# A hybrid decoder block with a PEER feed-forward on one core: six row buffers from the start, half-size weight loads, a first query projection in two pieces, and gate constants on early-free memory

## The chip, the cores and the metric

The kernel runs on one core of a Trainium2 chip. The metric is the device time in microseconds (us) of one launch. One launch was also profiled; its rows are quoted below. PE is the matmul engine (TensorE), DVE is VectorE, ACT is ScalarE, POOL is GpSimd and SP is SyncE, which here only issues transfers.

## The reference

One decoder block over 1024 tokens of width 1024: two token mixers (a stick-breaking attention and a gated delta net, 8 heads each) run on the normed input, are merged through sigmoid gates and go through an output projection into the residual stream. Then comes a PEER feed-forward: 16,384 single-neuron experts, addressed by two keys of 128 (e1 and e2).

```
h = rms_norm(x);  proj = h @ w_in
x = x + (sigmoid(gate_sb) * (o_sb @ w_branch_sb) + sigmoid(gate_gdn) * (o_gdn @ w_branch_gdn)) @ w_out
h2 = rms_norm(x)
q = h2 @ peer_w_q                                # 8 heads x 2 halves x 128
s1, s2 = q_half1 @ keys1.T, q_half2 @ keys2.T    # 128 scores each, top 16 of each
vals, c = top_k(s1 + s2, 16);  expert = e1 * 128 + e2;  gate = softmax(vals)
act = gelu(h2 . peer_u[expert]);  x = x + sum(gate * act * peer_v[expert])
```

Each token uses 8 x 16 = 128 experts. All of it is float32.

## The kernel before

**Tiling.** Tokens go in blocks of 128 and in two halves of four blocks (512 tokens). Float32 operands are split into a high and a low part (`split`: ACT makes the high part, DVE the low one), and each product is three matmuls (`mm3`, L72 to L74: high*high, high*low, low*high).

**Order.** Half 0, then half 1: `mixers` (attention heads, L295 to L317, then the delta net), gate logits, `merge`, `out_proj`, `ffn_norm` with `norm_T` (L678 to L686: norm a token block into `n_h`, transpose it on PE into `hf`), and `route` (per head: query projection `mm<-w,hf`, scores `pz<-keysT,r_q`, and on DVE a top 16 by `r_v`, `r_ix`). `route_block` turns the tops of a block into expert numbers and gates.

**Two ways for the experts.** Four of the eight token blocks go the dense way, the other four the gathered way.

- The *dense pass* handles four blocks (2, 3, 6, 7) against all experts: for each e1, `scores` (L885, L887: 128 experts' dot products on PE, then gelu), `weigh` (times the gate, into `d_a`), and on PE the products with the value rows `d_v` (`pz<-d_v,d_a`); after each four e1 and each half of the width DVE adds the sums to `d_acc` (L974). Its gates come from a *gate table* (`gate_table`): 64 steps of 8 tokens build a 128 x 128 gate matrix per token from one-hot tiles `gt_o`, and write it to memory as `g_d`. `gate_consts` makes a constant `gt_R` (4096 wide) and two small ones, `gt_L0` and `gt_L1`; the tile `gt_er` goes by DMA into `gt_L`, and PE multiplies `gt_R` by `gt_L` (L835).
- The *gathered* blocks (0, 1, 4, 5) fetch per token one row of 1024 floats for each of their 128 experts: POOL issues an indirect DMA (L1016, 128 tokens x 4 KB = 512 KB) into a row buffer `gb_row`, and DVE does one instruction of 1024 elements on it: a dot product for a `peer_u` row (L1019), a multiply-add into `gb_h` for a `peer_v` row (L1021). A block is 128 u rows and then 128 v rows; there are 1024 in all.

**What places the rows.** Rows of the first half's blocks can be gathered from half 1 on. `gather(phase)` is called at fixed places of each stage; it adds `PACE[phase]` to a count and creates as many row instructions as the count allows, at low priority: a scheduler puts every engine's instructions in order ahead of time, so a row may land later in DVE's order than its call. A row buffer is used in turn: four tiles, `gb_row0` to `gb_row3`; only in the dense pass two more are added (pool `gp2`). A row's DMA can start when DVE has finished the row that had the same buffer.

**Weights.** `load_w` brings 256 columns of a weight matrix as two DMAs of 512 KB (four blocks of 128 rows each) into `w_raw`, which has two buffers, and splits each in two steps (w_hi on ACT, w_lo on DVE). SP issues these loads in order, each when its buffer is free.

```
PACE = dict(sb=2.2, gdn=1.5, logits=2.5, merge=2.5, out=0.5, route=0, table=0.1, dense=5.25)
        self.due += PACE[phase]
        self.anchor = self.last_dve()
        with self.later(1000000):
            while self.due >= 1:
                self.due -= 1
                next(self.rows, None)
```

Of the kernel before, what the change touches and what calls it, by code (L numbers as in the profile page):

```python
# [30 lines left out]
PACE = dict(sb=2.2, gdn=1.5, logits=2.5, merge=2.5, out=0.5, route=0, table=0.1, dense=5.25)  # L31
# [7 lines left out]
class Block:  # L39
# [60 lines left out]
    def load_ba(self):  # L100

        hi, lo = [self.wp.tile([P, KD, CB], F32R, name=f"w_{a}")[:, :, 0:16] for a in ("hi", "lo")]
        raw = self.wraw.tile([P, 4, CB], F32, name="w_raw").rearrange("p a b -> p (a b)")[:, 0:16 * KD]
# [237 lines left out]
    def sb_pair(self, half, pair, kqv):  # L341
        nc = self.nc
        k, q, v = kqv
        for h in range(2):
            kts = [k[:, h, j * P:(j + 1) * P] for j in range(NTB)]
            vs = [v[:, j, h * P:(h + 1) * P] for j in range(NTB)]
            if half:
                ko = self.ch.tile([P, TH], F32, name="ko", bufs=2)
                nc.sync.dma_start(ko, self.k_old[pair][:, h])
                vo = self.ch.tile([P, NTB, P], F32, name="vo", bufs=2)  # L350
# [100 lines left out]
    def gdn_head(self, half, head, G, r):  # L451
# [247 lines left out]
    def route(self, half, hx, pool):  # L699
# [4 lines left out]
        for h in range(H):  # L704
            w = self.load_w(self.i["peer_w_q"], h * CB)
            q = []
            for t in range(2):
                ps = self.pmm.tile([P, TH], F32, name="mm")
                self.proj_T(ps, w, hx, t)
# [95 lines left out]
    def gate_table(self, n, blk, pool):  # L805
# [7 lines left out]
        tr = pool.tile([P, 3, P], F32, name="gt_tr", bufs=2)  # L813
        nc.scalar.copy(tr[:, 0:2], ps)
        nc.vector.tensor_scalar(tr[:, 2], tr[:, 1], -1.0, None, op0=OP.mult)
        er = pool.tile([P, 2, P], F32R, name="gt_er", bufs=2)
        nc.vector.tensor_scalar(er[:, 0], self.ef[blk][1], -64.0, None, op0=OP.add)
        nc.vector.tensor_tensor(er[:, 1], er[:, 0].bitcast(F32), er[:, 0].bitcast(F32), op=OP.mult)
# [360 lines left out]
```

## Time and profile before

| | |
|---|---|
| median of 3 runs | 3883.02 us (3879.04 to 3883.69) |
| the profiled execution | 3877.26 us, its span 3875.4 us |
| PE busy | 3596.4 us, 93% of the span |
| DVE busy | 3077.5 us, 79% |
| ACT busy | 1740.7 us, 45% |
| POOL busy | 1356.6 us, 35% |
| mean granted PE clock | 0.971 of full speed |
| data moved | 937.49 MB, 242 GB/s over the span; 536.94 MB of it by the gathered rows' queue |

Shares are of the whole span; the stages differ, and a table by stage stands first among the rows below; a window's row gives its start and end, its length, and the busy time of PE, PEld (PE's weight loads), DVE, ACT and POOL, each with its count of instructions. From 1010 us on the row gathering runs beside everything else. The stages, by the instructions that begin them: half 0 to 850 us, its norm and route to 1010, attention of half 1 to 1400, delta net to 1770, gate logits and merge to 1905, output projection and norm to 2010, route to 2127, gate table to 2400, dense pass to 3853, and a tail of last rows.

### The profile page before, as it was taken

To read this page: it belongs to the slowest core of one execution; us is meant where nothing else is said; L and a number is where in the kernel's file an instruction comes from. 1 tells how busy PE (TensorE), PEld (TensorE's weight loads), DVE (VectorE), ACT (ScalarE), POOL (GpSimd) and SP (SyncE) were. 2 spreads that over 40 slices of the span, in tenths; PEclk is the share of its full clock that TensorE was granted. 3 is DMA by queue.
4 is the path that set the end of the run, shared out by engine and by line. 5 is a ranking of instruction groups with operands and counts; after the bars stand their busy time and mean duration, and the time that the engine had idled before them with its cause. 6 is when DMAs were issued, how large, how long until landed. Compare 5 with 4: busy or idle time off the path is not lost.

```text
span 3875.4 us, 53560 instructions
## 1 busy us (share of the span) xinstructions
PE 3596.4 (93%) x18936; PEld 2983.8 (77%) x18936; DVE 3077.5 (79%) x6196; ACT 1740.7 (45%) x3846; POOL 1356.6 (35%) x1034
## 2 busy tenths in 40 slices
PE   8999999999999999998878877999999999999996
PEld 7878888788777688886667666787778787788785
DVE  5345554349988878888879998899898899899898
ACT  6755554333777655553322786222222322222221
POOL 0000000000044332223442003666666665676665
PEclk9999999999999999999989999999999999999998
DMA  4221113553377756558985568999999999999998
GB/s 121 88 82 50 55 50 115 174 186 93 96 256 265 246 191 192 191 182 290 325 307 170 158 185 289 353 361 358 334 365 358 345 371 365 348 364 374 353 359 312
DMA packets 344205, 937.49 MB, mean 242 GB/s; under 512 B 41984, under 2 KB 121088, under 8 KB 339712
## 3 DMA queue, kind: packets, MB, share of 16 engines
q0 software_dynamic: 147456, 536.94, 38.8%
q1 hardware_dynamic: 196480, 397.13, 30.1%
q8 instruction: 149, 2.44, 0.3%
q14 instruction: 120, 0.98, 0.1%
HBM read 864.22 MB, written 69.21 MB: 241 GB/s over the span
## 4 chain that ended last, share of the span: by engine, by line
PE 42%; issue 20%; POOL 12%; DVE 11%; DMA 10%; ACT 4%; SPq 0%; POOLq 0%; DVEq 0%; ACTq 0%
POOL gb_row L1016 12%; PE mm L72 6%; PE mm L74 6%; PE mm L73 6%; DMA gb_row<-peer_v,expert 5%; PE pc L848 3%; DMA gb_row<-peer_u,expert 3%; PE mm L885 2%; PE pz L532 2%; PE pz L526 2%; DVE gb_row L1019 2%; DVE w_lo L64 2%; PE mm L887 1%; PE pc L317 1%; PE pz L295 1%
## 5 line engine op out<-in xcount | busy, mean ns | idle before, releaser
L1016 POOL DMA_INDIRECT gb_row<-peer_u,expert x512 | 693.6, 1355 | 1848.2 <-DVE expert L793 1012.8
L1016 POOL DMA_INDIRECT gb_row<-peer_v,expert x512 | 661.9, 1293 | 656.4 <-DVE gb_h L1021 408.8
L1019 DVE SCALAR_TENSOR_TENSOR gb_row<-gb_row,gb_h 128x1024 f32<-128x1024 f32 x512 | 614.0, 1219 | 133.2 <-DMA gb_row<-peer_u,expert 109.7
L1021 DVE SCALAR_TENSOR_TENSOR gb_h<-gb_row,gb_act,gb_h 128x1024 f32<-128x1024 f32 x512 | 657.7, 1285 | 73.7 <-DMA gb_row<-peer_v,expert 50.4
L885 PE MATMUL mm<-hf,ut 128*128 128x512 f32 x2048 | 491.2, 391 | 6.9 <-DMA hf<-hd 6.9
L919 ACT CAST d_a<-u_act 128x512 fp32r<-128x512 f32 x128 | 79.2, 621 | 926.5 <-DVE u_act L915 917.7
L885 PEld LDWEIGHTS mm<-hf,ut 128*128 128x128 f32 x2048 | 386.1, 189 | 87.7 <-issue 7.6
L64 DVE TENSOR_TENSOR w_lo<-w_raw,w_hi 128x512 fp32r<-128x512 f32 (+1 forms) x450 | 297.6, 682 | 163.9 <-ACT w_hi L63 125.9
L63 ACT CAST w_hi<-w_raw 128x512 fp32r<-128x512 f32 (+1 forms) x450 | 262.1, 620 | 286.2 <-PE mm L73 122.6
L72 PE MATMUL mm<-h,w_hi 128*128 128x512 f32 (+1 forms) x784 | 322.9, 412 | 3.0 <-ACT pj L598 3.0
L74 PE MATMUL mm<-h,w_lo 128*128 128x512 f32 (+1 forms) x784 | 320.6, 409 | 0.0
L73 PE MATMUL mm<-h,w_hi 128*128 128x512 f32 (+1 forms) x784 | 319.7, 408 | 0.0
L72 PE MATMUL pz<-d_v,d_a 128*128 128x512 f32 x680 | 272.8, 401 | 41.2 <-DVE d_acc L974 30.1
L72 PE MATMUL mm<-w_hi,h 128*128 128x256 f32 x1024 | 299.8, 293 | 8.5 <-DVE x L647 5.7
L74 PE MATMUL mm<-w_hi,h 128*128 128x256 f32 x1024 | 294.0, 288 | 4.0 <-DVE h L64 4.0
L73 PE MATMUL mm<-w_lo,h 128*128 128x256 f32 x1024 | 295.1, 288 | 1.0 <-DVE w_lo L64 0.9
L74 PE MATMUL pz<-d_v,d_a 128*128 128x512 f32 x680 | 270.4, 398 | 0.0
L73 PE MATMUL pz<-d_v,d_a 128*128 128x512 f32 x680 | 270.4, 398 | 0.0
L887 PE MATMUL mm<-hf,ut 128*128 128x512 f32 x1024 | 257.0, 391 | 2.5 <-DVE ut L64 2.5
L887 PEld LDWEIGHTS mm<-hf,ut 128*128 128x128 f32 x1024 | 192.8, 188 | 42.8 <-DVE ut L64 3.3
L72 PEld LDWEIGHTS mm<-w_hi,h 128*128 128x128 f32 x1024 | 199.5, 195 | 16.3 <-DVE x L647 6.4
L73 PEld LDWEIGHTS mm<-w_lo,h 128*128 128x128 f32 x1024 | 199.7, 195 | 6.7 <-issue 3.8
(327 smaller groups left out, 7947.9 us busy)
## 6 DMA issues: line engine op xcount, KB each, us to landing
w_raw<-w_in SPq DMA_DIRECT2D x144, 512.0 KB
u_raw<-u_t SPq DMA_DIRECT2D x128, 512.0 KB
v_raw<-v_t SPq DMA_DIRECT2D x128, 512.0 KB
g_d<-gt_stg SPq DMA_DIRECT2D x16, 2048.0 KB
d_g<-g_d SPq DMA_DIRECT2D x31, 1024.0 KB
w_raw<-peer_w_q SPq DMA_DIRECT2D x32, 512.0 KB
gl<-pj SPq DMA_DIRECT2D x32, 256.0 KB
th<-gl SPq DMA_DIRECT2D x32, 256.0 KB
```

The lines of the kernel that those rows point to most:

```text
L63: nc.scalar.copy(hi, src)
L64: nc.vector.tensor_tensor(lo, src, hi.bitcast(F32), op=OP.subtract)
L72: mm(out, l[0], r[0], start=first, stop=False)
L73: mm(out, l[0], r[1], start=False, stop=False)
L74: mm(out, l[1], r[0], start=False, stop=last)
L848: self.last_gate = mm(pg[:, u - u0], o2[:, u], o1[:, u], start=True, stop=True)
L885: mm(ps, ut[0][:, k], hx[a][:, k, x0:], start=k + a == 0, stop=False)
L887: mm(ps, ut[1][:, k], hx[0][:, k, x0:], start=False, stop=k == KD - 1)
L919: nc.scalar.copy(hi, act)
L1016: nc.gpsimd.indirect_dma_start(out=r, out_offset=None, in_=self.i["peer_u" if p < n else "peer_v"][0], in_offset=bass.IndirectOffsetOnAxis ...
L1019: i = nc.vector.scalar_tensor_tensor(r, r, 1.0, h2, op0=OP.mult, op1=OP.mult, accum_out=act[:, q:q + 1])
L1021: i = nc.vector.scalar_tensor_tensor(acc, r, act[:, q:q + 1], acc, op0=OP.mult, op1=OP.add)
```

## The change

- **Pace.** New numbers: more rows are created in attention, delta net and table, fewer in logits, merge and the dense pass. Summed over the calls of half 1, 404.8 rows instead of 355.2 are due before the dense pass, and 620.8 instead of 672 in it. In DVE's order, though, 384 rows instead of 370 stand ahead of the first `d_acc` add.
- **Row buffers.** Six from the start instead of four, and two more in the dense pass.
- **Weights.** `load_w` makes four DMAs of 256 KB instead of two of 512 KB, with three buffers instead of two; what is loaded ahead is 768 KB instead of 1 MB.
- **Memory that pays for it.** `v_raw` moves from the pool `up` to `vp`, which opens only after the gate table; `ko` and `vo` have one buffer instead of two; `g_at` and `g_vn` reuse tiles; the residual block `x2[2]` is loaded after the merge instead of before.
- **Route.** For the first head of each half, `proj_T2` projects tokens 0 to 383 for both halves of the key, then tokens 384 to 511.
- **Gate table.** `gate_consts` and the first block's `gate_head` (transposes, `gt_tr`, `gt_er`) go into a pool of their own, `gk`, and are placed 2000 steps of priority earlier.

```
-PACE = dict(sb=2.2, gdn=1.5, logits=2.5, merge=2.5, out=0.5, route=0, table=0.1, dense=5.25)
+PACE = dict(sb=2.4, gdn=2.0, logits=2, merge=2, out=0.5, route=0, table=0.3, dense=4.85)
...
-        for k0 in range(0, KD, 4):
-            raw = self.wraw.tile([P, 4, CB], F32, name="w_raw")
-            self.nc.sync.dma_start(raw, src[c0 // CB][:, k0:k0 + 4])
-            for k in range(k0, k0 + 4, 2):
-                self.split(hi[:, k:k + 2], lo[:, k:k + 2], raw[:, k - k0:k - k0 + 2])
+        for k in range(0, KD, 2):
+            raw = self.wraw.tile([P, 2, CB], F32, name="w_raw")
+            self.nc.sync.dma_start(raw, src[c0 // CB][:, k:k + 2])
+            self.split(hi[:, k:k + 2], lo[:, k:k + 2], raw)
...
+    def proj_T2(self, outs, w, x):
+
+        for a, b in ((0, TH - P), (TH - P, TH)):
+            for j, out in enumerate(outs):
+                for k in range(KD):
+                    self.mm3(out[:, a:b], [v[:, k, j * P:(j + 1) * P] for v in w], [v[:, k, a:b] for v in x],
+                             k == 0, k == KD - 1)
...
-                ko = self.ch.tile([P, TH], F32, name="ko", bufs=2)
+                ko = self.ch.tile([P, TH], F32, name="ko", bufs=1)
...
-        at = W("g_at", bufs=1)
+        at = M
...
-        vn = W("g_vn", bufs=1)
+        vn = TN
...
-                ps = self.pmm.tile([P, TH], F32, name="mm")
-                self.proj_T(ps, w, hx, t)
+            pq = [self.pmm.tile([P, TH], F32, name="mm") for t in range(2)]
+            if h == 0:
+                self.proj_T2(pq, w, hx)
+            for t, ps in enumerate(pq):
+                if h:
+                    self.proj_T(ps, w, hx, t)
...
-                raw = up.tile([P, 2, 512], F32, name="v_raw")
+                raw = vp.tile([P, 2, 512], F32, name="v_raw")
...
-                self.gate_consts(gt)
+                with self.later(-2000):
+                    self.gate_consts(gk)
+                    head = self.gate_head(blks[0], gk)
...
-            gp2 = pool(name="gp2", bufs=1)
-            self.row_bufs += [(gp2, f"gb_row{4 + k}") for k in range(2)]
...
-        self.row_bufs = [(self.gp, f"gb_row{k}") for k in range(4)]
+        self.row_bufs = [(self.gp, f"gb_row{k}") for k in range(6)]
...
-        x2 = [xp.tile([P, D], F32, name=f"x2{tb}") for tb in range(3)]
+        x2 = [xp.tile([P, D], F32, name=f"x2{tb}") for tb in range(2)]
...
-                x2 += [fn.tile([P, D], F32, name=f"x2{tb}") for tb in range(3, NTB)]
+                x2 += [fn.tile([P, D], F32, name=f"x2{tb}") for tb in range(2, NTB)]
...
-            b.wraw = right("wraw", 2)
+            b.wraw = right("wraw", 3)
```

**DVE's order in the norm of half 1.** `n_h` is the normed second block (of `x21`), `hf1` the low part of the transposed blocks, `w_lo` the low part of the first query weights. Before, from the end of the second block's norm:

```order
2648 L682 SCALAR_TENSOR_TENSOR n_h_19375<-x21_17962,n_r_19379,ffnw_19343 128x1024
2649 L64 TENSOR_TENSOR w_lo_19479<-w_raw_19480,w_hi_19478 128x512
2650 L655 TENSOR_TENSOR x23_18853<-mm_19286,x23_18853 128x512
2651 L64 TENSOR_TENSOR hf1_19342<-pz1_19359,hf0_19341 128x4x128
2652 L64 TENSOR_TENSOR hf1_19342<-pz0_19366,hf0_19341 128x4x128
```

The same place with the change:

```order
2779 L689 SCALAR_TENSOR_TENSOR n_h_19923<-x21_18481,n_r_19927,ffnw_19891 128x1024
2780 L809 TENSOR_TENSOR gt_R_21110<-sel_402,selv_407 128x4096
2781 L813 TENSOR_SCALAR gt_L0_21112<-iota128_414 128x128
2782 L813 TENSOR_SCALAR gt_L1_21113<-iota128_414 128x128
2783 L825 TENSOR_SCALAR gt_er_21122<-ef2_1_417 128x128
2784 L662 TENSOR_TENSOR x23_19379<-mm_19829,x23_19379 128x512
2785 L826 TENSOR_TENSOR gt_er_21122<-gt_er_21122 128x128
2786 L64 TENSOR_TENSOR hf1_19890<-pz1_19907,hf0_19889 128x4x128
```

The constants `gt_R`, `gt_L0`, `gt_L1` and the tile `gt_er` now stand inside the norm chain, ahead of the last residual add (`x23`) and of the `hf1` of the first block; before, `gt_R` stood at row 2863 of DVE, in the middle of the route's last top 16.

**PE's order at the start of that route.** `pz<-ident,n_h` are the transposes of a normed block, `mm` a query projection. Before, all of the last two blocks' transposes (n_h_19405 and n_h_19435) stand ahead of the first projection:

```order
8194 L686 MATMUL pz1_19419<-ident_189,n_h_19405 128x128 x4
8195 L686 MATMUL pz0_19426<-ident_189,n_h_19405 128x128 x4
8196 L686 MATMUL pz1_19449<-ident_189,n_h_19435 128x128 x4
8197 L686 MATMUL pz0_19456<-ident_189,n_h_19435 128x128 x4
8198 L72 MATMUL mm_19492<-hf0_19341,w_hi_19478 128x512
8199 L72 MATMUL mm_19519<-hf0_19341,w_hi_19478 128x512
```

With the change, a few rows on (the third block's transposes are rows 8234 and 8235; n_h_19983 is the fourth block):

```order
8243 L72 MATMUL mm_20044<-hf0_19889,w_hi_20026 128x384
8244 L73 MATMUL mm_20044<-hf1_19890,w_hi_20026 128x384
8245 L74 MATMUL mm_20044<-hf0_19889,w_lo_20027 128x384
8246 L72 MATMUL mm_20044<-hf0_19889,w_hi_20026 128x384
8247 L73 MATMUL mm_20044<-hf1_19890,w_hi_20026 128x384
8248 L74 MATMUL mm_20044<-hf0_19889,w_lo_20027 128x384
8249 L693 MATMUL pz1_19997<-ident_189,n_h_19983 128x128 x4
8250 L693 MATMUL pz0_20004<-ident_189,n_h_19983 128x128 x4
8251 L72 MATMUL mm_20044<-hf0_19889,w_hi_20026 128x384
8252 L73 MATMUL mm_20044<-hf1_19890,w_hi_20026 128x384
```

Thirteen matmuls of 384 tokens (rows 8236 to 8248) now stand ahead of the fourth block's transposes; the 48 matmuls of 128 tokens come after all 48 of 384.

**PE's order at the start of the gate table.** `pz0<-keysT,r_q` is a route score, `mm<-hf,ut` a dense score of the first e1. Before, the last route score is row 8647, and 16 dense ones (rows 8650 to 8665) stand between it and the first product with `gt_R`; the last two of them and what follows:

```order
8663 L885 MATMUL mm_20914<-hf1_19342,ut0_20468 128x512
8664 L885 MATMUL mm_20914<-hf0_19341,ut0_20468 128x512
8665 L885 MATMUL mm_20914<-hf1_19342,ut0_20468 128x512
8666 L835 MATMUL pz1_20500<-gt_R_20479,gt_L0_20481 128x512
8667 L835 MATMUL pz1_20506<-gt_R_20479,gt_L0_20481 128x512
8668 L887 MATMUL mm_20914<-hf0_19341,ut1_20469 128x512 x2
8669 L848 MATMUL pc_20512<-gt_o1_20497,gt_o2_20499 128x128 x2
```

With the change:

```order
8735 L727 MATMUL pz0_21055<-keysT_19887,r_q_21026 128x128
8736 L851 MATMUL pz1_21131<-gt_R_21110,gt_L0_21112 128x512
8737 L851 MATMUL pz1_21137<-gt_R_21110,gt_L0_21112 128x512
8738 L820 MATMUL pz0_21581<-ident_189,ef3_0_418 128x128
8739 L820 MATMUL pz0_21581<-ident_189,gate3_427 128x128
8740 L864 MATMUL pc_21143<-gt_o1_21128,gt_o2_21130 128x128 x4
```

The table's first products follow the last route score directly, and its first transposes (of `ef2` and `gate2`) stand some ten rows further up, at 8727 and 8728.

## Rows read from the trace of the kernel before

**Rows 1.** Windows by stage: length, busy us (instructions) by engine, clock, DMA share, GB/s.

```profile
1010.00:1400.00 390.00, 359.76 (x1879) 276.85 (x1879) 336.00 (x731) 285.51 (x737) 153.64 (x132) 0.96 0.70 232
1400.00:1770.00 370.00, 359.51 (x2345) 309.63 (x2344) 308.18 (x684) 193.97 (x507) 105.11 (x96) 0.99 0.61 193
1770.00:1905.00 135.00, 115.24 (x455) 89.48 (x456) 110.82 (x202) 52.55 (x90) 46.88 (x36) 0.92 0.89 307
1905.00:2010.00 105.00, 74.73 (x494) 68.57 (x493) 81.89 (x154) 27.95 (x54) 40.94 (x36) 0.85 0.88 307
2010.00:2127.00 117.00, 109.03 (x522) 87.74 (x521) 111.39 (x527) 33.69 (x62) 31.23 (x25) 0.98 0.58 191
2127.00:2400.00 273.00, 216.64 (x1297) 179.97 (x1298) 251.63 (x591) 210.54 (x473) 45.20 (x31) 0.95 0.67 198
2400.00:3853.30 1453.30, 1389.46 (x6005) 1138.97 (x6003) 1321.01 (x1589) 394.61 (x507) 926.52 (x664) 0.98 0.95 356
```

**Rows 2.** Waits of the whole span: us in total, times, longest.

```profile
DVE gb_row L1019 <- DMA gb_row<-peer_u,expert: 109.7, 83, 5.1
DVE gb_h L1021 <- DMA gb_row<-peer_v,expert: 50.4, 43, 3.0
PE pz L72 <- DVE d_acc L974: 30.1, 14, 4.8
```

**Rows 3.** Waits in the attention of half 1, 1010 to 1400 us.

```profile
DVE gb_row L1019 <- DMA gb_row<-peer_u,expert: 38.6, 24, 3.5
PE pz L306 <- ACT sb_hi L63: 14.0, 4, 4.9
```

**Rows 4.** Waits in output projection and norm, 1905 to 2010 us.

```profile
DVE gb_row L1019 <- DMA gb_row<-peer_u,expert: 17.0, 12, 4.6
PE pz L686 <- DVE n_h L682: 10.9, 2, 7.7
PE pz L686 <- DVE rs_b L83: 10.4, 1, 10.4
```

**Rows 5.** Waits in the dense pass, 2400 to 3853.3 us.

```profile
DVE gb_row L1019 <- DMA gb_row<-peer_u,expert: 37.1, 35, 3.9
DVE gb_h L1021 <- DMA gb_row<-peer_v,expert: 22.3, 19, 2.1
```

**Rows 6.** Windows of four dense groups, from d_acc add to d_acc add.

```profile
2553.80:2599.80 46.00, 45.10 (x200) 37.01 (x199) 42.55 (x42) 12.27 (x16) 28.19 (x21) 1.00 0.99 373
2834.50:2881.90 47.40, 45.35 (x194) 37.03 (x193) 43.08 (x67) 12.48 (x16) 32.88 (x23) 0.97 0.96 361
3334.20:3390.20 56.00, 48.26 (x201) 38.84 (x200) 43.30 (x68) 12.28 (x17) 32.21 (x23) 0.93 0.90 345
3432.80:3476.60 43.80, 43.80 (x195) 36.27 (x194) 40.84 (x63) 13.14 (x17) 31.29 (x21) 1.00 0.99 379
```

**Rows 7.** DVE groups: count | busy, mean ns | idle before, releasers.

```profile
L1021 DVE SCALAR_TENSOR_TENSOR gb_h<-gb_row,gb_act,gb_h 128x1024 f32<-128x1024 f32 x512 | 657.7, 1285 | 73.7 <-DMA gb_row<-peer_v,expert 50.4 <-DMA gb_h<-x2d 15.9
L1019 DVE SCALAR_TENSOR_TENSOR gb_row<-gb_row,gb_h 128x1024 f32<-128x1024 f32 x512 | 614.0, 1219 | 133.2 <-DMA gb_row<-peer_u,expert 109.7 <-DMA gb_h<-h2d 20.0 <-issue 1.2
```

**Rows 8.** Timelines at the start of the gate table: DVE, PE, ACT.

```profile
2127.38 4.42 DVE L799 TENSOR_TENSOR gt_R<-sel,selv 128x4096 fp32r<-128x4096 f32 x1
2147.41 1.19 PE L835 MATMUL pz<-gt_R,gt_L 96*128 96x512 f32 x2 [10.17 <-DMA gt_L<-gt_er]
2148.55 2.90 ACT L839 ACTIVATE gt_o<-pz,gt_tr 128x128 f32<-128x128 f32 x8 [20.50 <-PE pz L835]
```

**Rows 9.** Timeline of PE, 128-wide products late in the gate table.

```profile
2373.99 2.05 PE L848 MATMUL pc<-gt_o,gt_o 128*128 128x128 f32 x16 [0.94 <-ACT gt_o L842]
```

**Rows 10.** Timeline of PE at the norm of half 0.

```profile
857.00 3.91 PE L686 MATMUL pz<-ident,n_h 128*128 128x128 f32 x16 [7.72 <-DVE rs_b L83]
```

**Rows 11.** Weight loads on SP: count, issue time in ns (min/median/max).

```profile
L95 SPq DMA_DIRECT2D w_raw<-w_in x144: 327/328/928, 3.3 to 1796.2; - x144
L95 SPq DMA_DIRECT2D w_raw<-peer_w_q x32: 327/328/360, 827.1 to 2098.4; - x32
```

More of the change, by code (lines that the diff above doesn't have):

```diff
@@ L102, in load_ba @@
         hi, lo = [self.wp.tile([P, KD, CB], F32R, name=f"w_{a}")[:, :, 0:16] for a in ("hi", "lo")]
-        raw = self.wraw.tile([P, 4, CB], F32, name="w_raw").rearrange("p a b -> p (a b)")[:, 0:16 * KD]
+        raw = self.wraw.tile([P, 2, CB], F32, name="w_raw").rearrange("p a b -> p (a b)")[:, 0:16 * KD]
         raw = raw.rearrange("p (k n) -> p k n", k=KD)
@@ L347, in sb_pair @@
             if half:
-                ko = self.ch.tile([P, TH], F32, name="ko", bufs=2)
+                ko = self.ch.tile([P, TH], F32, name="ko", bufs=1)
                 nc.sync.dma_start(ko, self.k_old[pair][:, h])
-                vo = self.ch.tile([P, NTB, P], F32, name="vo", bufs=2)
+                vo = self.ch.tile([P, NTB, P], F32, name="vo", bufs=1)
                 nc.sync.dma_start(vo, self.v_old[pair][:, :, h * P:(h + 1) * P])
@@ L706, in route @@
             q = []
-            for t in range(2):
-                ps = self.pmm.tile([P, TH], F32, name="mm")
-                self.proj_T(ps, w, hx, t)
+            pq = [self.pmm.tile([P, TH], F32, name="mm") for t in range(2)]
[4 more added lines that the diff above has]
+                    self.proj_T(ps, w, hx, t)
                 qt = pool.tile([P, TH], F32, name="r_q", bufs=3)
@@ L803, in gate_consts, with gate_head @@
             nc.vector.tensor_scalar(L, self.iota128, 0.0, 1.0, op0=OP.mult, op1=OP.add)
-    def gate_table(self, n, blk, pool):
-        nc, mm = self.nc, self.nc.tensor.matmul
+    def gate_head(self, blk, gk):
+        nc = self.nc
         ps = self.pzt([P, 2, P])
@@ L812, in gate_table @@
             nc.tensor.transpose(ps[:, a], src, self.ident)
-        tr = pool.tile([P, 3, P], F32, name="gt_tr", bufs=2)
+        tr = gk.tile([P, 3, P], F32, name="gt_tr", bufs=2)
         nc.scalar.copy(tr[:, 0:2], ps)
         nc.vector.tensor_scalar(tr[:, 2], tr[:, 1], -1.0, None, op0=OP.mult)
-        er = pool.tile([P, 2, P], F32R, name="gt_er", bufs=2)
+        er = gk.tile([P, 2, P], F32R, name="gt_er", bufs=2)
         nc.vector.tensor_scalar(er[:, 0], self.ef[blk][1], -64.0, None, op0=OP.add)
         nc.vector.tensor_tensor(er[:, 1], er[:, 0].bitcast(F32), er[:, 0].bitcast(F32), op=OP.mult)
+        return tr, er
+    def gate_table(self, n, blk, pool, head):
+        nc, mm = self.nc, self.nc.tensor.matmul
+        tr, er = head
         R = 8
@@ L941, in dense @@
                     nc.sync.dma_start(hx[a][:, :, x0 + n * P:x0 + (n + 1) * P].bitcast(F32), self.hd_d[blk][a])
-            with self.tc.tile_pool(name="gt", bufs=1, reuse_waits="tile") as gt:
-                self.gate_consts(gt)
+            with self.tc.tile_pool(name="gt", bufs=1, reuse_waits="tile") as gt, \
+                    self.tc.tile_pool(name="gk", bufs=1, reuse_waits="tile") as gk:
+                with self.later(-2000):
+                    self.gate_consts(gk)
+                    head = self.gate_head(blks[0], gk)
                 for n, blk in enumerate(blks):
@@ L946, in dense @@
                         routes[blk - NTB]()
-                    self.gate_table(n, blk, gt)
+                    self.gate_table(n, blk, gt, head if n == 0 else self.gate_head(blk, gk))
                     if n < nb - 1:
@@ L1076, in half @@
             with tp("fn") as fn:
-                x2 += [fn.tile([P, D], F32, name=f"x2{tb}") for tb in range(3, NTB)]
+                x2 += [fn.tile([P, D], F32, name=f"x2{tb}") for tb in range(2, NTB)]
                 if x2_in is None:
-                    self.load_x(half, x2, range(3, NTB))
+                    self.load_x(half, x2, range(2, NTB))
                     self.out_proj(half, mg, x2)
```

1 line of the change is left out of this document (removed).

## The prediction

> **What bounds the kernel now.** I read the table by stage first [rows 1]: in each row PE's busy time against the length, then the DMA share. In attention and delta net PE works 359.8 of 390 and 359.5 of 370 us, in the dense pass 1389.5 of 1453.3, so the bound is PE with small holes. The large holes lie between: 19.8 us at logits and merge (135.0 less 115.2), 30.3 at output projection and norm (105.0 less 74.7, clock 0.85), 56.4 in the gate table. The PE idle time of the seven stages sums to 219 us (30.2 + 10.5 + 19.8 + 30.3 + 8.0 + 56.4 + 63.9); what the change can win there lies in it.
>
> Next the waits of the whole span [rows 2]. DVE stands on the row transfers themselves for 109.7 us (u rows, 83 times) and 50.4 us (v rows, 43 times): its next instruction is a row whose 512 KB are not there yet, and everything behind it in DVE's fixed order waits too. That matters only where PE or the chain needs what is queued behind. In attention it does: 38.6 us of DVE standing, and PE waits 14.0 us in four pieces for the split score tile behind it [rows 3]. At output projection and norm it is 17.0 us, beside PE's 10.9 and 10.4 us on the norm chain, which runs on DVE [rows 4]. In the dense pass DVE stands 37.1 and 22.3 us on rows [rows 5], so some 100 of the 160 us fall before it, and PE waits 30.1 us in all for `d_acc` adds [rows 2].
>
> Last I compared single dense groups [rows 6]; POOL's count is the rows issued. A group of 21 u rows with PE never idle takes 43.8 us, at DMA share 0.99 and 379 GB/s. With 21 v rows it takes 46.0, with 23 u rows 47.4, and where a block begins 56.0. So a group has a PE floor of 43.8 us, and over some 20 rows it is a matter of transfers and DVE (42.6 and 43.1 us busy).
>
> **The change part by part.**
>
> *Six buffers ahead of the dense pass.* A row's transfer starts when the row with the same buffer is done; with six, five rows of DVE work instead of three lie between. In attention I return most of PE's 14.0 us: −10. Bounds: 0 (the waits only move) and −20 (two thirds of PE's 30.2 us of idle time, if the added slack also helps the other engines). In delta net, merge and output projection PE's idle time is 10.5 and 19.8 us in the two windows [rows 1] and row waits are a part of it: −7, bounds 0 and −14. Against it stands the new pace: about 14 to 18 rows more before the dense pass, at 1.22 to 1.29 us each [rows 7], some 20 us of DVE. DVE is busy 336 of 390 and 308 of 370 us [rows 1], so they fit where it stood waiting; without that cover they cost up to those 20 us.
>
> *Norm and route of half 1.* The chain is DVE's. Of the 17.0 us of row waits [rows 4] I take half as lying in it: −9. The new order has four rows fewer there (15 before, 11 now, from the last residual add but one to the last `hf`): −4.9 at 1.22. Into it move `gt_R`, 4.42 us [rows 8], and four small instructions, about 1 us together: +5.5. The split projection lets PE begin with three blocks. In half 1 PE waited 10.4 us for the third block's norm and less for the fourth's; what it can use is at most the fourth block's share, about 4 us, and I take −2.5, less the cost of small matmuls. These replace 48 matmuls of 512 columns by 48 of 384 and 48 of 128. A 128-wide one is bounded below by a quarter of a 512-wide one (43.8 us for 195 matmuls, 0.225, so 0.056) and above by the gate table's products, 16 in 2.05 us, 0.128 [rows 9]: 0 to 48 x 0.072 = 3.5 us; I take 1, nearer to the lower end, since those products wait on ACT. Then two rows more land before the route ends, +2.4, where DVE is busy 111.4 of 117 us [rows 1]. Sum −9 − 4.9 + 5.5 − 2.5 + 1 + 2.4 = −7.5, say −7; bounds +4 (no wait returned) and −15.
>
> The Trainium skill (TensorE: Matmul & The Clock Gate, Back-to-back issue gap) gives about 81 ns for each 128-wide matmul in a stream with weight loads; by it that one cost would be 48 x (0.081 − 0.056) = 1.2 us, an estimate. No row here has such a float32 matmul.
>
> *Half 0's norm.* There the third and the fourth block's transposes run as one piece of 3.91 us after 7.72 us of idling [rows 10]. Starting after the third block saves at most half the piece: −2, bounds 0 and −3.5 (the small matmuls again against it).
>
> *Table start.* PE idles 10.17 us for `gt_L`'s transfer, ACT 20.50 us for PE's first product [rows 8]; ACT paces the table, so its standing is the loss. With the constants early and 16 dense scores out of the way, the first product can follow the last route score. But the first `gt_o1` still comes behind the route's top 16 on DVE, and the two halves of the work (38 top-16 instructions, rows) are only rearranged: −9, bounds 0 and −20.5.
>
> *Dense pass.* Before it 384 rows are done instead of 370: 14 fewer, 18 us of DVE and 7.3 MB, at 360 GB/s 20 us of transfers. But their spread changes: by DVE's order five groups now carry 23 or 24 u rows (the seventh to the eleventh), the later ones mostly 19 or 20 instead of 21 or 22. By the groups of 23 and of 21, u rows over 21 cost (47.4 − 43.8)/2 = 1.8 us each at most [rows 6], so these five groups cost, against the 23 that stood there, +5 to +9; some 20 later groups fall toward the floor, v groups by 1.5 us (46.0 to about 44.5, ten of them, −15), u groups hardly; and the block switch of 56.0 us eases by about 5. Sum 7 − 15 − 5 = −13, I take −12. Bounds: +8 (the heavy groups cost, the light ones were at the PE floor) and −30.
>
> *Tail and the rest.* Ten rows after the last add instead of eleven: −1.5. `v_raw` is no longer loaded during the table, so the first values come later: +2, bounds 0 and +8 (two loads of 512 KB at 360 GB/s are 3 us, and the split behind them). One `ko` and `vo` buffer, reused `g_at` and `g_vn`, `x2[2]` loaded later: 0, since PE's order around them is the same; if that cover fails, each head pays a load of 256 KB in its chain, about 1 us by the same rate, eight times.
>
> *Weights in halves.* 224 more loads: 144 + 32 [rows 11] and 48 for the other three matrices. I put 0: they are issued far ahead, and PE's waits for weights are hidden behind matmuls of the chunk before. Without that cover, each extra issue holds SP for 0.328 us [rows 11].
>
> **The sum.** −10 − 7 − 7 − 2 − 9 − 12 − 1.5 + 2 = −46.5 from the profiled 3877.3: 3830.8. The median of the runs stands 5.8 above the profiled one (3883.0), so 3836; I say 3835. Taking the bounds as independent (half-widths 10, 7, 10, 2, 10, 19, 4) gives about 27 us either way: 3808 to 3862 for this case.
>
> **Rivals.**
>
> *A. Route and dense eat it (0.13).* The norm chain takes the constants and the rows and returns no wait (+4), the table starts no sooner since DVE's top 16 is what it waited for (0), the heavy groups cancel the light ones (0), and attention and mixers win as forecast: −10 − 7 + 4 − 2 − 1.5 + 2 = −14.5, so 3877.3 − 14.5 + 5.8 = 3869. For it: DVE is full in the route, 111.4 of 117 [rows 1]. Against it: ACT's 20.50 us [rows 8] end with PE's product, and not with DVE.
>
> *B. Slower (0.07).* Weight loads of half the size become the bound. If each of the 224 extra issues delays the split that PE waits for by its 0.328 us, that is +73: 3835 + 73 = 3908. It decides from 0.25 us each on, since 224 x 0.25 = 56 brings it over 3891. For it: 768 KB ahead instead of 1 MB, with the DMA share at 0.89 and 0.88 in merge and norm [rows 1]. Against it: the same bytes, and three buffers that come free in smaller steps. The Trainium skill (DMA: Bandwidth & Descriptors, Bandwidth) says to batch transfers to 1 MiB or more; this is the rule that speaks against the change. No run here shows its size yet, and the gathered rows of 512 KB reach 379 GB/s together [rows 6], well short of such a batch.
>
> *C. The buffers don't end the waits (0.12).* Rows are late because the transfers share the bandwidth, and more in flight only makes each later. Then attention and mixers give 0, norm and route 0, while table (−9), half 0 (−2), dense (−6, half of the forecast), tail and `v_raw` remain: −16.5, so 3867. For it: the DMA share is 0.70 in attention and near 0.9 after it [rows 1]. Against it: 232 GB/s there, while 379 are reached [rows 6].
>
> **How the numbers follow.** The forecast has 0.60, A 0.13, B 0.07, C 0.12, and 0.08 is for a larger gain (below 3808, chiefly in the dense pass). The range 3805 to 3872 holds the forecast, A, C and a part of the larger gain, and leaves out B. A measurement of this kernel tells 0.2%, 8 us, from no change: faster is below 3875, slower above 3891. Faster: 0.60 + 0.08 + 0.08 of A + 0.09 of C = 0.85; same 0.08; slower 0.07.
>
> **What would show it.** Right: DVE's waits on rows before the dense pass fall from some 100 us to under 20; PE's four gaps at L306 go; ACT stands at most 12 us at the table start; groups of 19 or 20 rows take 43.5 to 44.5 us, those of 24 take 47.5 to 50. Wrong: ACT's `w_hi` waits on `w_raw` transfers grow and PE waits behind them (B); row waits stay near 100 us with the DMA share up (C); the norm chain or the table start is as long as before (A); or the groups of 24 rows pass 52 us, and the dense pass gets longer.

## The result and the profile after

The changed kernel takes 3917.48 us (median of six runs, 3906.38 to 3920.20) against 3877.79 for the kernel before (six runs): the ratio is 1.0095, with a 95% interval of 1.0076 to 1.0115. The forecast was 3835 and faster; it is slower, by 39.7 us between the medians (37 by the ratio), and past the upper end of the range. The profiled execution has a span of 3915.6 us.

I cut both traces at the same instructions (the same nth matmul of the same name), so that a stage's length can be compared. First the kernel before, then the changed one; the columns are start:end, length, busy time of PE, PEld, DVE, ACT and POOL with counts, granted clock, DMA share, GB/s. The five windows are: end of the delta net with the gate logits of half 0; the attention of half 1; the last delta-net head with the logits of half 1; the gate table; the dense pass.

```profile
538.70:701.90 163.20, 163.06 (x939) 136.31 (x938) 70.97 (x175) 85.37 (x213) 0.00 (x0) 1.00 0.37 116
1027.10:1321.00 293.90, 272.67 (x1435) 203.88 (x1434) 253.68 (x508) 235.30 (x621) 114.88 (x100) 0.96 0.70 230
1723.10:1811.40 88.30, 77.87 (x361) 61.66 (x360) 72.01 (x174) 38.79 (x93) 31.26 (x25) 0.94 0.88 300
2147.40:2379.80 232.40, 191.55 (x1196) 160.32 (x1196) 220.31 (x498) 200.23 (x459) 30.68 (x22) 0.97 0.66 188
2458.40:3852.60 1394.20, 1341.06 (x5802) 1100.29 (x5802) 1274.69 (x1523) 376.81 (x484) 898.04 (x644) 0.98 0.95 355
```

```profile
534.30:714.50 180.20, 168.24 (x954) 140.19 (x955) 69.50 (x172) 81.92 (x209) 0.00 (x0) 0.97 0.34 101
1049.00:1356.10 307.10, 280.06 (x1432) 206.24 (x1431) 262.47 (x523) 236.04 (x623) 129.86 (x108) 0.94 0.70 234
1761.80:1866.00 104.20, 79.62 (x362) 63.54 (x361) 83.67 (x180) 33.11 (x85) 38.06 (x31) 0.90 0.77 257
2191.70:2431.20 239.50, 193.93 (x1215) 161.57 (x1214) 234.95 (x584) 202.26 (x464) 27.56 (x20) 0.97 0.69 196
2502.60:3894.40 1391.80, 1341.70 (x5836) 1103.54 (x5834) 1262.03 (x1494) 378.87 (x484) 886.62 (x631) 0.98 0.95 352
```

The logits of half 0 grew by 17.0 us (163.2 to 180.2), those of half 1 by 15.9, the attention by 13.2; the gate table by 7.1. The dense pass shrank by 2.4 from its first `d_acc` add on, and by 9.6 from the end of the table. What stands between the windows: half 0's norm and route lost 3.8, the input norm behind them 8.5, the stretch from the attention to the delta net 4.6, merge and output projection of half 1 12.7; its norm won 6.9 and its route lost 8.4. Between the last route score and the table's first product stood 24.5 us, and all of it is gone. So all of the loss lies ahead of the dense pass, in stages that were to win or to stay the same.

The waits of the whole span of the changed kernel answer to [rows 2] (L1035 and L1037 are L1019 and L1021 of before):

```profile
ACT w_hi L63 <- DMA w_raw<-w_in: 131.9, 53, 9.3
...
ACT w_hi L63 <- DMA w_raw<-peer_w_q: 98.2, 23, 12.2
...
DVE gb_row L1035 <- DMA gb_row<-peer_u,expert: 61.6, 58, 2.8
...
PE mm L72 <- ACT o L63: 44.9, 9, 13.2
...
DVE gb_h L1037 <- DMA gb_row<-peer_v,expert: 18.9, 19, 2.2
```

Three rows of the kernel before that [rows 2] does not show:

```profile
ACT w_hi L63 <- DMA w_raw<-w_in: 47.1, 18, 7.4
ACT w_hi L63 <- DMA w_raw<-peer_w_q: 43.4, 14, 6.4
...
PE mm L72 <- ACT o L63: 11.5, 6, 6.7
```

The waits of the changed kernel's attention in half 1 answer to [rows 3]:

```profile
DVE gb_row L1035 <- DMA gb_row<-peer_u,expert: 7.7, 12, 1.2
PE pz L313 <- ACT sb_hi L63: 9.3, 5, 3.2
```

DVE's standing on row transfers fell as forecast: from 160.1 to 80.5 us in all, in attention from 38.6 to 7.7. PE's gaps at the score tile shrank only from 14.0 to 9.3. What grew is ACT's wait for weight transfers: `w_hi` waits 131.9 us on `w_raw` from `w_in` and 98.2 on the query weights, where the trace before shows 47.1 and 43.4. And a wait that was 11.5 us before is now 44.9: PE for the merge's split tile `o`.

The dense groups answer to [rows 6]: 24 u rows, 20 v rows, 19 u rows.

```profile
2942.00:2990.80 48.80, 45.61 (x193) 37.29 (x192) 44.69 (x69) 12.49 (x16) 32.81 (x24) 0.95 0.97 367
3260.40:3303.80 43.40, 43.40 (x193) 35.95 (x192) 41.60 (x41) 13.33 (x16) 27.13 (x20) 1.00 0.97 367
3439.70:3485.00 45.30, 43.81 (x194) 35.96 (x193) 38.60 (x60) 12.05 (x16) 27.24 (x19) 1.00 0.94 341
```

The group of 20 rows takes 43.4 us and that of 19 takes 45.3; the one of 24 takes 48.8: inside what was forecast for them, or near it. It is the shortest of the five heavy groups, though. By the first `d_acc` add of each group, three others take 49.8 to 50.3. The first, with which a block begins, takes 57.8, over the 52 named as a sign of being wrong; with the group ahead of it, it takes 99.5 us, where the two around that switch took 98.0 before. At the other switch two groups take 92.2 us for 97.1. The dense pass as a whole did not get longer.

### The profile page after: what moved, and what is told of

It is laid out like the page before. It is cut to its first block, busy times and chain, and to the rows that moved or that the text cites. A ratio compares the mean times of both kernels' runs of the same rounds, so it can differ in the third digit from the quotient of the medians.

```text
span 3915.6 us, 54293 instructions
## 1 busy us (share of the span) xinstructions
PE 3608.1 (92%) x19032; PEld 2998.9 (77%) x19032; DVE 3080.4 (79%) x6196; ACT 1743.1 (45%) x3845; POOL 1373.6 (35%) x1034
## 3 DMA queue, kind: packets, MB, share of 16 engines
q0 software_dynamic: 147456, 536.94, 38.6%
## 4 chain that ended last, share of the span: by engine, by line
PE 34%; issue 23%; DVE 13%; POOL 13%; DMA 11%; ACT 5%; SPq 0%; POOLq 0%; DVEq 0%; ACTq 0%
POOL gb_row L1032 13%; PE mm L72 6%; PE mm L73 6%; PE mm L74 6%; DMA gb_row<-peer_v,expert 3%; DMA w_raw<-w_in 2%; PE pc L864 2%; PE pz L539 2%; PE pz L533 2%; DVE gb_h L1037 2%; DVE gb_row L1035 2%; DVE w_lo L64 1%; PE pz L529 1%; PE pz L302 1%; PE pc L324 1%
## 5 line engine op out<-in xcount | busy, mean ns | idle before, releaser
L1032 POOL DMA_INDIRECT gb_row<-peer_v,expert x512 | 672.0, 1313 | 644.7 <-DVE gb_h L1037 434.0
L1037 DVE SCALAR_TENSOR_TENSOR gb_h<-gb_row,gb_act,gb_h 128x1024 f32<-128x1024 f32 x512 | 658.5, 1286 | 48.8 <-DMA gb_h<-x2d 21.9
L1035 DVE SCALAR_TENSOR_TENSOR gb_row<-gb_row,gb_h 128x1024 f32<-128x1024 f32 x512 | 611.4, 1221 | 77.6 <-DMA gb_row<-peer_u,expert 61.6
L63 ACT CAST w_hi<-w_raw 128x512 fp32r<-128x512 f32 (+1 forms) x450 | 269.9, 620 | 472.2 <-DMA w_raw<-w_in 131.9
L903 PEld LDWEIGHTS mm<-hf,ut 128*128 128x128 f32 x1024 | 192.3, 188 | 39.5
L72 PEld LDWEIGHTS mm<-w_hi,h 128*128 128x128 f32 x1024 | 202.3, 198 | 23.1 <-issue 7.8
L74 PEld LDWEIGHTS mm<-w_hi,h 128*128 128x128 f32 x1024 | 202.2, 198 | 7.0 <-DVE h L64 4.1
```

The lines of the kernel that those rows point to most:

```text
L63: nc.scalar.copy(hi, src)
L72: mm(out, l[0], r[0], start=first, stop=False)
L74: mm(out, l[1], r[0], start=False, stop=last)
L903: mm(ps, ut[1][:, k], hx[0][:, k, x0:], start=False, stop=k == KD - 1)
L1032: nc.gpsimd.indirect_dma_start(out=r, out_offset=None, in_=self.i["peer_u" if p < n else "peer_v"][0], in_offset=bass.IndirectOffsetOnAxis ...
L1035: i = nc.vector.scalar_tensor_tensor(r, r, 1.0, h2, op0=OP.mult, op1=OP.mult, accum_out=act[:, q:q + 1])
```

## The experiments

Each is timed against the kernel before on the same chip (3874.6 to 3880.4 us there); times are medians, ratios are to the kernel before with their 95% interval. Theory 1, formed on the traces above, has two parts: the merge's first loads are issued too late, and less weight is loaded ahead. Its rival is that the size or the number of the loads costs the time; a second one that the new pace or the row buffers do.

**e1: the late `o_raw`.** SP issues in a fixed order. In half 0 before, the first `o_raw` loads stand ahead of the first branch weights:

```profile
653.02 1.90 SPq L612 DMA_DIRECT2D o_raw<-osb  x3
...
686.50 3.83 SPq L95 DMA_DIRECT2D w_raw<-w_branch_sb  x2
```

In the changed kernel they stand behind eleven of those weight loads, each of which waits for a free buffer:

```profile
702.95 1.53 SPq L95 DMA_DIRECT2D w_raw<-w_branch_sb  x3
707.42 0.33 SPq L95 DMA_DIRECT2D w_raw<-w_branch_sb  x1
707.84 1.33 SPq L619 DMA_DIRECT2D o_raw<-osb  x3
```

and PE waits for what they bring, in half 0 and in half 1 (in brackets the idle time before the instruction, and what ended it):

```profile
713.19 0.80 PE L72 MATMUL mm<-o,w_hi 128*128 128x512 f32 x1 [11.43 <-ACT o L63]
...
1864.57 1.22 PE L72 MATMUL mm<-o,w_hi 128*128 128x512 f32 x2 [13.22 <-ACT o L63]
```

The data were not late: the attention's results `osb`, which these loads read, were last written at 244 us, and the delta net's by 646. What changed is memory: in the built program the merge's tiles end at byte 114368 of each partition, and the pool `pj`, in which the logits' buffers lie, begins at 113920. Before, the merge ended at 106176. The 8 KB of two row buffers push the merge up, and the last `th` tile overlaps the pool by 448 bytes. The experiment takes one `th` buffer away; the tiles then end at 112320.

```
-                    th = pool.tile([P, TH], F32, name="th", bufs=4)
+                    th = pool.tile([P, TH], F32, name="th", bufs=3)
```

> The changed kernel with three th buffers in the merge instead of four, and nothing else. Theory 1: the six row buffers push the merge's tiles up by 8 KB, so that the last th tile overlaps the buffers of the gate logits by 448 bytes; the order of SP then puts the merge's first o_raw loads behind the weight loads of the logits and of the first branch, and PE waits for o. With three th buffers the tiles end below, the loads stand ahead again: PE's wait for o falls from 44.9 to about 12 us, and the time by about 33 us (17.0 in half 0 and 15.9 in half 1), to some 3885. Rival 2: the half-size weight loads are what PE waits behind; then the time stays within 8 us of 3917, and a th buffer less can only cost.

Measured: 3893.29 us, ratio 1.0035 (1.0021 to 1.0050): 24.2 us less than the changed kernel. In the built order `o_raw` stands first again, and PE's wait for `o` is down to 8.6 us:

```profile
PE mm L72 <- ACT o L63: 8.6, 4, 5.5
```

So the late loads are shown, at some 24 us and not 33. The kernel is still 15 us slower than before, and more than 15 us of loss is left to explain, since other parts of the change win time.

**e2: the half-size weight loads alone.** The `load_w` part of the diff on the kernel before:

```
-        for k0 in range(0, KD, 4):
-            raw = self.wraw.tile([P, 4, CB], F32, name="w_raw")
...
+        for k in range(0, KD, 2):
+            raw = self.wraw.tile([P, 2, CB], F32, name="w_raw")
...
-            b.wraw = right("wraw", 2)
+            b.wraw = right("wraw", 3)
```

> The kernel before with only the weight loads halved (256 KB, three buffers). Theory 1: the loads alone cost little in the merge, since o_raw stays ahead; the attention and delta net of half 1 and the route pay for 256 KB less loaded ahead, 0 to +15 us. Rival 2 (the halves are the whole loss): +35 to +55 us, and ACT's waits for w_raw transfers double as in the changed kernel (47 to 132 us from w_in).

Measured: 3935.85 us, 1.0143 (1.0123 to 1.0163). Alone they cost 57.8 us, more than the whole change. `o_raw` is early here. Waits of its span:

```profile
DVE w_lo L64 <- ACT w_hi L63: 224.0, 109, 8.2
ACT w_hi L63 <- DMA w_raw<-w_in: 119.4, 51, 9.4
...
ACT w_hi L63 <- DMA w_raw<-peer_w_q: 89.7, 27, 7.5
...
PE mm L72 <- ACT w_hi L63: 17.5, 8, 3.9
```

ACT's waits for weight transfers have more than doubled, as in the changed kernel. The expectation of theory 1 for this run (0 to 15 us) was far off, that of its rival (35 to 55) nearly right. The loss lies where weights are loaded: at the table's first product this kernel is 55 us behind the one before (2202.5 for 2147.41 us), and its dense pass, from the first `d_acc` add to the last, takes 1398.4 us for 1394.2. PE itself stands on `w_hi` for only 17.5 us. DVE, whose fixed order holds `w_lo` among everything else, waits for `w_hi` far longer than before:

```profile
DVE w_lo L64 <- ACT w_hi L63: 125.9, 61, 8.8
```

How the rest reaches PE was not followed wait by wait.

**e5: the same loads, with four buffers.** The same edit with `right("wraw", 4)`: as many loads of the same size as in e2, but 1 MB ahead as before.

> The kernel before with weight loads of 256 KB and four buffers, so that 1 MB is loaded ahead as before. If the 57 us of the three-buffer kernel come from the 256 KB less ahead: within 10 us of the kernel before, and ACT's waits for w_raw from w_in back to some 50 us. If they come from the number of loads (each takes 3.2 us to land, where one of twice the size takes 4.2): 35 to 60 us slower than before.

Measured: 3879.80 us, 0.9995 (0.9982 to 1.0009): no difference.

```profile
DVE w_lo L64 <- ACT w_hi L63: 136.8, 64, 8.8
...
ACT w_hi L63 <- DMA w_raw<-peer_w_q: 45.8, 18, 8.5
...
ACT w_hi L63 <- DMA w_raw<-w_in: 29.0, 21, 4.9
```

So neither the number nor the size of the loads costs anything here. The sources of e2 and e5 differ in the fourth buffer alone (which also moves the tiles beside it by 2 KB), and the waits that differ are ACT's for these very loads and DVE's behind them: what cost 57.8 us is that 768 KB instead of 1 MB were on their way or waiting. The scheduler reckons with the buffers, so the built orders differ too (SP's in 276 of 1016 places); how much of the 57.8 us comes by the order was not taken apart.

**e3 and e6: fewer row buffers.** The changed kernel has six row buffers throughout and adds none in the dense pass, so there it has as many as the kernel before. In e3 it has four ahead of the dense pass and six in it; in e6 it has five throughout, and the weight loads of before.

```
-        self.row_bufs = [(self.gp, f"gb_row{k}") for k in range(6)]
+        self.row_bufs = [(self.gp, f"gb_row{k}") for k in range(4)]
...
+            gp2 = pool(name="gp2", bufs=1)
+            self.row_bufs += [(gp2, f"gb_row{4 + k}") for k in range(2)]
...
+            del self.row_bufs[4:]
```

> The changed kernel with four row buffers ahead of the dense pass and six in it, as before; all else as changed. Theory 1: the merge gets its o_raw early again, minus 33 us, while DVE stands on row transfers again (some 100 us before the dense pass, which cost PE some 14 us in attention): about 3890. Rival 2: the loss stays, 3910 to 3930, since the buffers were only a gain.

> The changed kernel with five row buffers instead of six, and weight loads of 512 KB in two buffers as before; the merge's tiles then end below the logits' buffers with four th. If the half-size loads (57 us alone) and the late o_raw (24 us) are the whole loss and the rest is a gain: gate constants minus 11, dense pass and mixers with five buffers minus 15 to minus 30, so 3835 to 3855. Rival: five buffers or the new pace lose as the four did (3980), then 3880 or more.

Measured: 3980.10 us, 1.0262 (1.0242 to 1.0283), and 3970.70 us, 1.0238 (1.0216 to 1.0261). Both theories missed e3; e6 fell to its rival, that five buffers or the new pace lose as the four did. Up to the end of the gate table e6 is ahead of the kernel before by 26 us; it loses 119 after it. e3 is 37 us behind there, and loses another 56 in the dense pass. The first two dense groups of e6 and a later one of 24 u rows:

```profile
2439.20:2497.10 57.90, 45.17 (x193) 36.98 (x193) 31.91 (x46) 12.04 (x16) 19.32 (x13) 0.88 0.61 210
2497.10:2550.40 53.30, 47.29 (x196) 37.77 (x196) 33.80 (x40) 15.34 (x19) 18.97 (x14) 0.96 0.66 239
2895.90:2946.60 50.70, 45.48 (x193) 37.16 (x193) 44.72 (x70) 12.27 (x16) 32.75 (x24) 0.94 0.96 353
```

The first two take 57.9 and 53.3 us and carry only 13 and 14 rows, and in them (2440 to 2555 us) DVE stands on row transfers:

```profile
DVE gb_row L1036 <- DMA gb_row<-peer_u,expert: 39.2, 12, 5.9
```

The likely reason stands in DVE's order. In both kernels the last ten or so u rows of the second gathered block all use one buffer (in e6 `gb_row4`, ten rows one after the other; in e3 `gb_row0`), because the scheduler had skipped that buffer for a while, so that each row's transfer begins when the row before it is done. The rows that are missed there crowd the later groups, 22 to 24 in most; in e6 these have five buffers, where before there were six, and take 47 to 53 us. No run mends the order alone, so this reason is argued and not shown, and how much of the 119 us belongs to the skipped buffer and how much to five buffers is open.

**e4: the early gate constants alone.** The `gate_consts`, `gate_head` and `gk` parts of the diff on the kernel before.

```
+                with self.later(-2000):
+                    self.gate_consts(gk)
+                    head = self.gate_head(blks[0], gk)
```

> The kernel before with only the gate constants and the first gate head early. If the shorter table start of the changed kernel (24 us less between the last route score and the table's first product, some 7 of it given back in the table) comes from this part: minus 12 to minus 18 us against the kernel before. If it came from the row buffers or the pace: within 5 us of it.

Measured: 3866.58 us, 0.9965 (0.9954 to 0.9976): 11.5 us faster, just short of the 12 to 18 expected. PE's first product and ACT's first `gt_o` there, against 2147.41 and 2148.55 in [rows 8]:

```profile
2122.25 0.80 PE L841 MATMUL pz<-gt_R,gt_L 96*128 96x512 f32 x2
...
2128.16 2.90 ACT L845 ACTIVATE gt_o<-pz,gt_tr 128x128 f32<-128x128 f32 x8 [2.96 <-DVE gt_tr L813]
```

The changed kernel shows the same, its last route score at 2191.7:

```profile
2191.72 0.79 PE L851 MATMUL pz<-gt_R,gt_L 96*128 96x512 f32 x2
...
2198.42 2.90 ACT L855 ACTIVATE gt_o<-pz,gt_tr 128x128 f32<-128x128 f32 x8 [2.96 <-DVE gt_tr L823]
```

PE starts the table at once; ACT then waits for `gt_tr` from DVE, and not for PE. In e4 PE's first product comes 25 us earlier than before and ACT's first `gt_o` 20; the table takes 6.3 us longer, so that 19 are left at its end. (The launch that was profiled took 3860.56 us, 6 less than the median.)

**e7: the old pace.** The changed kernel with the `PACE` line of before.

```
+PACE = dict(sb=2.2, gdn=1.5, logits=2.5, merge=2.5, out=0.5, route=0, table=0.1, dense=5.25)
```

> The changed kernel with the old pace numbers. If the new pace is right for six buffers: slower than the changed kernel or the same, 3917 to 3935, the dense pass longer by some 10 us again. If the extra rows before the dense pass crowd DVE there: faster, 3895 to 3910, with attention and norm shorter.

Measured: 3923.74 us, 1.0113 (1.0092 to 1.0133), which cannot be told from the changed kernel's 1.0095. The new pace neither made the loss nor won much.

**e8: the split query projection alone.** The `proj_T2` part of the diff on the kernel before.

```
+            if h == 0:
+                self.proj_T2(pq, w, hx)
```

> The kernel before with only the first query projection in two pieces. Predicted: minus 2 in half 0 and minus 1.5 in half 1, so 0 to minus 4 us, within what can be told. If the 48 matmuls of 128 columns cost more than reckoned, plus 3 to plus 8.

Measured: 3885.30 us, 1.0018 (1.0007 to 1.0028): 7 us slower, the upper case. Half 0's route at the change from 384 to 128 columns, and its end:

```profile
867.67 0.34 PE L73 MATMUL mm<-hf,w_hi 128*128 128x384 f32 x1
867.85 0.34 PE L74 MATMUL mm<-hf,w_lo 128*128 128x384 f32 x1
...
873.10 0.28 PE L73 MATMUL mm<-hf,w_hi 128*128 128x128 f32 x1
873.22 0.27 PE L74 MATMUL mm<-hf,w_lo 128*128 128x128 f32 x1
875.75 0.71 PE L728 MATMUL pz<-keysT,r_q 128*128 128x128 f32 x4 [2.26 <-ACT r_q L722]
```

From 867.85 to 868.02 a 384-wide matmul takes 0.173 us; between 868.08 and 873.22 the 128-wide ones follow at 0.11, nearly half of what one of 512 takes (0.233 in the same place before). 48 x (0.173 + 0.11) is 13.6 us where 48 x 0.233 was 11.2: 2.4 us more each half. And both halves of the projection now end together, so PE waits 2.26 us for ACT's copy to `r_q`, which before ran beside the second projection. Starting early did not pay for it: in half 0 all four blocks' transposes stand ahead of the projection in this kernel's order, and norm and route together take 125.3 us for 121.3; in half 1 the fourth block's stand behind the first products, as in the changed kernel, and the two take 145.4 for 139.8.

**e9, e10, e12, e11: room made for all of it.** The changed kernel with 1 MB of weights ahead and early `o_raw`. The room is taken from tiles that are short-lived; e9 has four buffers of 256 KB, e10 two of 512 KB, e12 is e10 without the split projection, and e11 is e12 with the room for the input norm taken from `r_q`.

```
-            lo = pool.tile([P, TH], F32R, name="sb_lo", bufs=3)
+            lo = pool.tile([P, TH], F32R, name="sb_lo", bufs=2)
...
-            R = pool.tile([P, P], F32, name="g_R")
+            R = pool.tile([P, P], F32, name="g_R", bufs=1)
...
-                raw = pool.tile([P, TH], F32, name="o_raw", bufs=3)
+                raw = pool.tile([P, TH], F32, name="o_raw", bufs=2)
...
-                    th = pool.tile([P, TH], F32, name="th", bufs=4)
+                    th = pool.tile([P, TH], F32, name="th", bufs=3)
...
-                        self.norm_in(1, hx, nin)
+                        self.norm_in(1, hx, nin, 1)
```

(`g_o1` and `g_u` lose a buffer as `g_R` does; e11 has `r_q` with two buffers in place of the last edit.)

> The changed kernel with four weight buffers of 256 KB (1 MB ahead, as before) and its o_raw loads early again. The room comes from one buffer less of g_R, g_o1, g_u, sb_lo, o_raw, th and of the second half's input tiles. If the 256 KB less ahead (57 us alone) and the late o_raw (24 us) are the changed kernel's whole loss, the rest is the gain that was forecast: 3917 - 24 - 57 = 3836, 3825 to 3855 with what the single buffers cost. If the row buffers and the pace bring nothing beside the gate constants (12 us): 3860 to 3875.

> As the run with four buffers of 256 KB, but with two of 512 KB as in the kernel before. The bytes ahead are the same, and the runs with the loads alone showed no cost of the halved size at equal bytes; so within 8 us of that run. A difference beyond it, either way, would belong to the load size (a load of 256 KB lands in 3.2 us, one of 512 KB in 4.2) or to the order of SP that comes with it.

> As the run with two weight buffers of 512 KB and room made, without the split query projection and nothing else. By the run of the split alone (plus 7 us): 3845, 3840 to 3850. If the split is only bad where the norm of half 0 is undisturbed: 3852 as with it.

> As the run with two weight buffers of 512 KB and room made, without the split query projection, and with the room for the second half's input norm taken from r_q (two buffers instead of three) where that run had one input tile instead of two. In that run the half-0 norm and the input norm of half 1 ended 20 us late, about 10 of it made up later. If the single input tile was the cause: minus 10 to minus 15 us, and the split projection alone cost 7: some 3832 to 3840. If two r_q buffers hold up the route's query projections: up to plus 15 in the two routes, and 3845 to 3860.

| kernel | us | ratio to before |
|---|---|---|
| e9, four buffers of 256 KB | 3859.28 | 0.9940 (0.9916 to 0.9964) |
| e10, two buffers of 512 KB | 3852.01 | 0.9922 (0.9897 to 0.9947) |
| e12, e10 without the split | 3832.03 | 0.9892 (0.9865 to 0.9918) |
| e11, e12 with room from `r_q` | 3844.46 | 0.9926 (0.9900 to 0.9953) |

e9 and e10 ran on one chip, e12 and e11 on another, so ratios are to be compared. The best beats both kernels, the one before by 1.1% and the changed one by some 2.0% (0.9892 / 1.0095). e9 and e10 cannot be told apart, which repeats e5. e9 came out just above its expected range and at the edge of its rival's (3860 to 3875), so by itself it does not decide between them. e12 is below its range of 3840 to 3850: by the ratios 12 us less than e10, where the split alone had cost 7, though the intervals overlap. e11 lies between its two cases and decides neither. e12 and e11 have intervals that overlap, so where the room for the input norm is best taken is open. Waits of e12's span, the last row from the list of PE alone:

```profile
DVE gb_row L1025 <- DMA gb_row<-peer_u,expert: 56.9, 50, 4.5
...
ACT w_hi L63 <- DMA w_raw<-w_in: 30.0, 11, 6.6
...
PE mm L72 <- ACT o L63: 19.6, 7, 8.5
...
PE pz L306 <- ACT sb_hi L63: 0.9, 1, 0.9
```

ACT's wait for `w_in` weights is 30.0 us instead of 131.9, PE's for `o` is 19.6 instead of 44.9, and DVE's waits on u rows stay low. PE's waits at the score tile, 14.0 us before and 9.3 in the changed kernel, are now 0.9 us, and the attention of half 1 (from the first `pc<-sb_a` product to the last) takes 286.9 us, where it took 297.8 before and 312.3 with the change.

## Why the prediction was wrong

The step that failed is "Weights in halves". I put 0 for it: "they are issued far ahead, and PE's waits for weights are hidden behind matmuls of the chunk before." Alone it measured +57.8 us (e2). Being far ahead was the cover that I named, and the edit took a quarter of it away. Rival B had the place, but its price counted the extra issues, and 224 more loads cost nothing where 1 MB stays ahead (e5); the 768 KB stood in it only as an argument. That its +73 and its 3908 lie near the +57.8 and the 3917 is luck. The rule of the Trainium skill that I weighed there (DMA: Bandwidth & Descriptors, Bandwidth: batch to 1 MiB or more) would have had e5 slower than the kernel before; its ratio is 0.9995.

A second term was missing. I put the memory edits at 0 "since PE's order around them is the same", and looked at the tiles that the diff names. Two row buffers moved the merge's tiles over the logits' pool by 448 bytes, SP's order changed, and the first loads of both merges went behind the weight queue: +24.2 us (e1).

Third, a size: the split projection, with half 0's norm, was −2 − 2.5 + 1 and measured some +7 (e8). A 128-wide matmul takes 0.11 us, near the upper bound of 0.128 that I had, and I took a value near the lower one; the wait for `r_q` I had not seen.

A reading was wrong too: of the two windows from which I took −7 for delta net, merge and output projection, neither holds the output projection.

What held: DVE's waits on rows fell ahead of the dense pass from some 100 us to 20 (80.5 less 46.8 and 13.6 in the dense pass), and in attention to 7.7. The gate constants won, in the place that was named: 17 us of trace from the table's start to its end in the changed kernel (24.5 less 7.1) for −9, and 11.5 alone. The dense pass shrank by 9.6 us for −12, the tail by 1.6 for −1.5. Attention's −10 became +13.2, with the row waits gone: there ACT waits 43.2 us for `w_in` weights, where it had waited 18.6. With 1 MB ahead (e12) the attention is 10.9 us shorter than before, and PE's waits at the score tile are all but gone, which fits the term. The stages from the attention's end to the output projection, −7, lost 32 (4.6 − 1.0 + 15.9 + 12.7), and norm and route of half 1, also −7, came out at +1.5.

The parts, each measured by itself where it was: +57.8 (loads), +24.2 (late `o_raw`), +7.8 (split) and −11.5 (constants) make +78.3; the changed kernel is +39.7. So −39 would be left for the six buffers, the pace and the dense pass together; the forecast's own terms for these sum to −39.5 (the −46.5, without −9 for the table, −2 and −2.5 + 1 for the split and +5.5 for the constants in the norm). This is a remainder and not a measurement of its own, since parts need not add, and e3 and e6 show how far they can fail to. Runs with several parts together give less. From e1 to e9 and e10, with early `o_raw` in all three, 1 MB ahead for 768 KB brings 37 and 44 us by the ratios, and not 57.8. What is left in e9 and e10 besides split and constants is some −20 and −27, and some −30 in e12 (−42 less the −11.5 of the constants), each with what the single buffers cost. By these runs the gain is there and smaller than forecast. No run has the six buffers alone; e7 gives the pace little of it. That e12 came out at 3832, beside the 3835 forecast for the change, is partly luck: it leaves out the split, and against the kernel before on its chip (3874.6) it is −42, where −48 had been forecast from 3883.0.

## What to carry to other kernels

When memory is taken from a buffer that loads ahead, count the bytes that stay ahead and not the loads: here 768 KB for 1 MB cost 57.8 us alone, and twice as many loads of half the size cost nothing. A tile that grows moves others, and one of them may come to lie over memory of another stage and wait for it: look up who shares its bytes, and compare the order of the queue that fills it, also in stages that the diff does not name. With a split, price the small matmuls by the nearest rows of that size, and look at what used to run beside the second half.

## What the runs showed of the hardware

Landing times of the weight loads, e2 with 256 KB (columns: count, KB each, median us from issue to landing):

```profile
w_raw<-w_in SPq DMA_DIRECT2D x288, 256.0 KB, 3.2
w_raw<-peer_w_q SPq DMA_DIRECT2D x64, 256.0 KB, 4.0
```

and e4 with 512 KB:

```profile
w_raw<-w_in SPq DMA_DIRECT2D x144, 512.0 KB, 4.2
w_raw<-peer_w_q SPq DMA_DIRECT2D x32, 512.0 KB, 4.5
```

Half the bytes land in three quarters of the time or more (3.2 for 4.2 us). If the time were a fixed part and one by bytes, the fixed part of `w_in` loads would be, as an estimate, 2 x 3.2 − 4.2 = 2.2 us, and that of `peer_w_q` loads 2 x 4.0 − 4.5 = 3.5; the medians come from two kernels with different traffic beside the loads. The Trainium skill (DMA: Bandwidth & Descriptors, Anatomy of one DMA) gives about 2.0 us fixed for a DMA that GpSimd issues; of these loads, which SP issues, those of `w_in` come out close to it and those of `peer_w_q` do not. With a fixed part in each landing, fewer bytes on their way move fewer per second; this fits e2, but no run here took it apart further.

In half 0's route, at a granted clock of 1.00, float32 matmuls of 128 columns followed at 0.11 us and those of 384 at 0.173 (e8), those of 512 at 0.233 (the kernel before): a third of the columns takes nearly two thirds of the time. The Trainium skill (TensorE: Matmul & The Clock Gate, Back-to-back issue gap) has about 81 ns for 128 columns; the measured 0.11 us decides here.
